# Two value-projection chunks side by side at the opening of a float32 decoder trunk, and layer 0's bias bands and residual on the weights' DMA queue

## The chip, the core and the metric

The kernel runs on one core of one Trainium2 chip. The metric is the device time of one execution in microseconds, as the median of three runs. The engines are called as the profile calls them: PE (TensorE; PEld is its weight load), ACT (ScalarE), DVE (VectorE), POOL (GpSimd) and SP (SyncE, which only issues DMAs here). A q behind an engine's name stands for its sequencer.

## The reference

One sequence of T = 256 tokens, width 2048, float32 throughout, two layers. Layer 0 has full causal attention (with 256 tokens its block-sparse form has one block), layer 1 has sliding-window attention (128 keys) with sinks and four shared key/value heads. Both add a T5 relative-position bias to the scores, and both are followed by a gated feed-forward network with a causal convolution of width 3. Each block is closed by a residual with a LayerNorm.

```python
for layer in range(2):
    if layer == 0:
        attn = moba_attention(h, moba_w_qkv[0], moba_w_o[0], rel_bias)     # 16 heads of 128
    else:
        k_band, v_band = shared_kv_bands(h, swa_w_kv)                      # 4 kv heads
        attn = swa_attention(h, swa_w_q[0], swa_sinks[0], swa_w_o[0], k_band, v_band, band_bias, band_mask)
    h = layer_norm(ALPHA * h + attn, ln_g[layer, 0], ln_b[layer, 0])
    ffn = conv_ffn(h, ffn_w_up[layer], ffn_conv_w[layer], ffn_conv_b[layer], ffn_w_down[layer])
    h = layer_norm(ALPHA * h + ffn, ln_g[layer, 1], ln_b[layer, 1])
```

The few words on the change say "layer 1's value projection" and count layers from 1; in the code it is `l == 0`, and this text says layer 0.

## The kernel before, in words

All weights lie in one DRAM tensor `wst`, cut into "halves" of 128 partitions x 1024 float32 (512 KB), in the order in which PE uses them. `load_weights` (L98) issues the next half on SP's queue into one of four `raw` buffers. A half then is split: ACT copies it to `wh` in the rounded type float32r (L128), DVE subtracts to get the low part `wl` (L157). `wh` and `wl` have four buffers each. Matmuls then add high times high, high times low and low times high, which keeps float32's accuracy. `split_upto` (L159) does the splits up to a given half, and at the end of each one issues the next raw load, which has to wait until the split has freed its buffer. `pieces` (L95) says whether a half is loaded and split whole or in two pieces of 512 columns: before, only half 0 is in pieces.

The order of work is written out by hand. `take` (L203) hands out the next half: it first runs the splits up to three halves ahead, then the jobs on an agenda (`at(n, f, ...)` puts a job n halves ahead). `step` (L197) counts one half on, and runs jobs that PE itself has (`pe_at`). So each engine's queue holds its instructions in this order and runs them in order; DMAs of SP stand in SP's order, DMAs of POOL in POOL's.

Two ways of multiplying are used. A feature unit (`ws_unit`, L293) has weights as the stationary operand: two halves, 16 K-blocks of 128, one accumulator bank of PSUM (L300 and L303). A `Moving` chunk (L337) has weights as the moving operand: 512 output columns, 16 K-blocks of 128 x 512, i.e. eight halves, with two accumulators (one for each 128 tokens) and three matmuls for each block and token tile (L353 to L355). PSUM has four `acc` banks and four `at` banks.

Layer 0's attention (L768 to L775) goes in four groups of four heads. A group begins with `v_group` (L743), the value projection of 512 columns as one `Moving` chunk, whose accumulators are evacuated into `vt` (two buffers). Then, for each head, come two feature units (q and k) and the softmax steps, which are spread over the following halves (L695 to L701).

The opening (`load_input`, L216): the input, transposed, is loaded in blocks `xc` and split into `xT`, high and low. Blocks 0 and 1 are loaded one by one on ACT's queue beside the two pieces of half 0, the others in pairs on SP's queue between the raw loads. All four tables of the bias (`bias_table`, L264) are loaded on SP as well; at half 3 PE makes the bias rows from them (L275), and POOL writes these to `ud` in DRAM (L278). `spread_bias` (L282) copies `ud` from DRAM to DRAM, with overlapping rows, into bands of four heads of 128 x 256 (512 KB each), and `load_bias` (L287) brings a band into SBUF. Both are on POOL's queue, for layer 0 at halves 4, 12, 20 and 28, and a load waits for its spread. The residual `res` (two loads of 1 MB, L244) and the LayerNorm vectors `gb` (two of 1 MB, L421) are on POOL's queue too, behind them. A tile has to be free and its data landed before an instruction that uses it runs; the framework puts in those waits, and at most eight DMAs of SP are under way, since the ninth waits for the first's semaphore.

Of the kernel before, what the change touches and what calls it, by code (L numbers as in the profile page):

```python
# [18 lines left out]
P = 128  # L19
T = 256  # L20
D = 2048
KB = D // P
# [15 lines left out]
RAW_BUFS = 4  # L38
HALF_BUFS = 4
AHEAD = HALF_BUFS - 1  # L40
HW = 1024
# [5 lines left out]
OPENING = 4  # L47
PAIRS = 6
LEAD = (16, 0)
GROUPS = ((6, 6, 6, 6, 6, 6), (6, 4, 4, 4, 4, 4))  # L50


# [25 lines left out]
def trunk(ctx: ExitStack, tc: tile.TileContext, wst, xT_in, x_in, relb, onehot, umask, sinks, conv_in, ln_g, ln_b, out):  # L78
    nc = tc.nc
# [13 lines left out]
    reach, placed = {}, {}  # L93

    def pieces(u):  # L95
        return (slice(0, HW // 2), slice(HW // 2, HW)) if u == 0 else (slice(0, HW),)

    def load_weights(behind=None):  # L98
        u = todo["load"]
        if u < n_halves:  # L100
            raws[u] = wpool.tile([P, HW], F32, name="raw")
            for j, c in enumerate(pieces(u)):
                nc.sync.dma_start(raws[u][:, c], wst[u][:, c])
                if behind:
                    behind(j)
            todo["load"] += 1
# [52 lines left out]
    def split_upto(i, behind=None):  # L159
        while todo["low"] <= min(i, n_halves - 1):  # L160
            s = todo["low"]
            high_upto(s, behind)
            if s in quad:
                quad_low(s)
                raws.pop(s - 1)
                load_weights()
            elif len(pieces(s)) == 1:
                if s - 1 in quad:
                    q = quad[s - 1]
                    nc.scalar.activation(q.uh, q.tm[:, 512:], AF.Copy)  # L170
                low_piece(s, slice(0, HW))
                if s - 1 in quad:
                    minus(q.ul, q.tm[:, 512:], q.uh.bitcast(F32))
            placed.pop(s)
            todo["low"] += 1
            if s + 1 not in quad:
                raws.pop(s)
                load_weights()
# [4 lines left out]
    def at(n, f, *a, first=False):  # L183

        fs = before.setdefault(slot["now"] + n, [])
        fs.insert(0 if first else len(fs), (f, a))
# [29 lines left out]
    def load_input(pool, tables):  # L216
        xc = pool.tile([P, KB, T], F32, name="xc", bufs=1)

        def load_x(k, n=2):
            (nc.scalar if n == 1 else nc.sync).dma_start(xc[:, k:k + n], xT_in[:, k:k + n, :])  # L220

        def split_x(k, n=2):
            ks = slice(k, k + n)
            nc.scalar.activation(xT[:, ks, 0:T], xc[:, ks], AF.Copy)
            nc.vector.tensor_tensor(out=xT[:, ks, T:2 * T], in0=xc[:, ks], in1=xT[:, ks, 0:T].bitcast(F32),
                                    op=ALU.subtract)

        load_weights(lambda j: load_x(j, 1))
        for c in range(1, RAW_BUFS):
            load_x(2 * c)  # L230
            load_weights()
        tables()
        load_x(2 * RAW_BUFS)
        split_upto(0, lambda j: split_x(j, 1))
        for c in range(1, KB // 2):
            if c + RAW_BUFS < KB // 2:
                load_x(2 * (c + RAW_BUFS))
            if c < HALF_BUFS:
                split_x(2 * c)
                split_upto(c)  # L240
            else:
                at(c - HALF_BUFS, split_x, 2 * c)

    def load_residual():  # L244
        for t in range(2):
            nc.gpsimd.dma_start(res[:, t, :], x_in[t * P:(t + 1) * P, :])

    at(24, load_residual)

    ident = const.tile([P, P], F32, name="ident")  # L250
    make_identity(nc, ident)
# [29 lines left out]

    def spread_bias(l, h0, h1):  # L282
        a = ud[l, h0:h1, :]
        nc.gpsimd.dma_start(band[l, h0:h1], bass.AP(tensor=a.tensor, offset=a.offset + P - 1,
                                                    ap=[[UL, h1 - h0], [-1, P], [1, 2 * P]]))

    def load_bias(bias, l, h0, h1):  # L287
        nc.gpsimd.dma_start(bias[:, h0:h1, :], band[l, h0:h1].rearrange("h q j -> q h j"))

    def cols(w, j):  # L290
        return w[:, j * P:(j + 1) * P]
# [411 lines left out]
    def layer_attention(l, rest, stage, turnover):  # L703
        oT = st
        kept = []
        if l:
            norm, turned = rest
            turn, low = turned
            n0 = nexth["i"]
            c = COLS[1]  # L710
            norm(c[0])
            norm(c[1])
            split_upto(n0 + 7)
            norm(c[2])

            def early(t, i):
                if t == 0 and i == 5:
                    pts = [turn(c[j]) for j in range(2)]
                    low(c[0], pts[0])
                    norm(c[3])  # L720
                    low(c[1], pts[1])
                if t == 0 and i == 7:
                    low(c[2], turn(c[2]))
                if t == 1 and i == 1:
                    low(c[3], turn(c[3]))
                if t == 1 and i < HALF_BUFS:
                    split_upto(n0 + 8 + i)

            kept = [acc_tile(), acc_tile()]
            Moving(lambda k: xT[:, k, :], KB).chunk(kept, early=early)  # L730
        pool = stage(f"att{l}")
        bias = pool.tile([P, NH, 2 * P], F32, name="bias", bufs=1)
        if l == 0:
            load_input(pool, lambda: bias_table(pool))
        else:
            nc.vector.tensor_scalar(nsk, sk, -1.0, None, op0=ALU.mult)
        for i, h in enumerate(range(0, NH, 4)):
            n = (4 + 8 * i, 4 * i)[l]
            if l == 0:
                at(n, spread_bias, l, h, h + 4)  # L740
            at(n, load_bias, bias, l, h, h + 4)

        def v_group(accs=None):  # L743
            if not accs:
                accs = [acc_tile(), acc_tile()]
                Moving(lambda k: xT[:, k, :], KB).chunk(accs)
            vt = pool.tile([P, 2, 512], F32, name="vt", bufs=1 if l else 2)

            def evac():
                for t in range(2):  # L750
                    nc.scalar.activation(vt[:, t, :], accs[t], AF.Copy)

            at(0, evac)
            return vt

        def feat_unit(name, bufs):
            acc = acc_tile()
            ws_unit(acc)
            o = pool.tile([P, T], F32, name=name, bufs=bufs)

            def evac():
                nc.scalar.activation(o, acc[:, T:2 * T], AF.Copy)
                nc.vector.tensor_tensor(out=o, in0=acc[:, 0:T], in1=o, op=ALU.add)

            at(0, evac, first=True)
            return o

        if l == 0:  # L768
            for g in range(NH // 4):
                vt = v_group()  # L770
                for j in range(4):
                    h = 4 * g + j
                    q = feat_unit("qT", 4)
                    k = feat_unit("kT", 4)
                    attention(pool, l, h, q, vt[:, :, j * P:(j + 1) * P], k, bias, oT)  # L775
        else:
            vt = v_group(kept)
            ks = [feat_unit("kT", KVH) for _ in range(KVH)]
            for h in range(NH):
                q = feat_unit("qT", 4)  # L780
                j = h // GRP
                attention(pool, l, h, q, vt[:, :, j * P:(j + 1) * P], ks[j], bias, oT)
        return project_out(lambda k: oT[:, k, :], NH, 2 * l, turnover.homes, AF.Gelu_apprx_tanh, turnover)
# [134 lines left out]
    return b.transpose(0, 2, 1, 3).reshape(-1, P, HW)  # L918


def _paired(w):

    b = w.reshape(FT, P, NCH // 2, 2, 512).transpose(2, 0, 3, 1, 4)
    seq = np.stack([b[n, k, c] for n in range(NCH // 2) for k, c in paired_order(LEAD[n], GROUPS[n])[0]])
    return seq.reshape(-1, 2, P, 512).transpose(0, 2, 1, 3).reshape(-1, P, HW)


def _stream(w_qkv, w_o0, w_kv, w_q, w_o1, w_up, w_down):
    parts = []
    q, k, v = (w_qkv[:, i * D:(i + 1) * D] for i in range(3))  # L930
    for g in range(4):
        c = slice(512 * g, 512 * (g + 1))
        parts.append(_moving(v[:, c]))
        parts.append(np.stack([_still(q[:, c]), _still(k[:, c])], 1).reshape(-1, P, HW))

    def ffn(l):
        up = w_up[l]
        parts.append(np.stack([_still(up[:, :DFF]), _still(up[:, DFF:])], 1).reshape(-1, P, HW))
        parts.append(_paired(w_down[l]))

    parts.append(_moving(w_o0))
    ffn(0)
    parts.append(_moving(w_kv[:, 512:]))
    parts.append(_still(w_kv[:, :512]).reshape(-1, P, HW))
    parts.append(_still(w_q).reshape(-1, P, HW))
    parts.append(_moving(w_o1))
    ffn(1)
    return np.concatenate(parts, 0)
# [36 lines left out]
```

## Time and profile before

| | |
|---|---|
| median of three runs | 2074.63 us (2074.5 to 2076.37) |
| the profiled execution | 2074.71 us, its span 2072.7 us |
| busy share of the span | PE 99%, PEld 86%, DVE 76%, ACT 50%, POOL 1% |
| data moved by DMA | 405.10 MB, mean 195 GB/s |
| of it on SP's queue (q1) and POOL's (q0) | 383.67 MB and 19.33 MB |
| granted TensorE clock | 0.998 of full speed |

How to read it: all times within the profile count from the span's start. A row of the timeline has the start, the busy time, engine, line, operation, output<-inputs, and in brackets the idle time of the engine ahead of it with what ended that. A row of waits has the time in all, how often, and the longest. A matmul's busy time is longer than the distance to the next one's start, since matmuls overlap in the array, so a stall of PE is read from the starts.

### The profile page before, as it was taken

The numbers are of one execution on the slowest core, as the hardware profiler recorded it, in microseconds if no ns is written. First come the engines' busy times: TensorE is split into PE (matmuls) and PEld (weight loads), VectorE is DVE, ScalarE is ACT, GpSimd is POOL, SyncE is SP. The second block draws the span as 40 slices with busy tenths as digits, with TensorE's granted clock in tenths as the row PEclk, the third lists the DMA queues.
The fourth block names the chain that finished last, engine by engine and source line by source line (L and its number), as shares of the span: only waits on it lengthen the run. The fifth ranks groups of instructions, "written<-read, shape, count | busy, mean of one in ns | idle before, by whom it ended". The sixth has DMA issues, their size and how long they took to land.

```text
span 2072.7 us, 28857 instructions
## 1 busy us (share of the span) xinstructions
PE 2058.5 (99%) x11004; PEld 1779.1 (86%) x11004; DVE 1575.2 (76%) x2310; ACT 1031.2 (50%) x1453; POOL 23.3 (1%) x36
## 2 busy tenths in 40 slices
PE   9999999999999999999999999999999999999997
PEld 7888888988888888888888888898888888888886
DVE  5555556787877877898986676788787787788886
ACT  5444444444545555454553555445545454555452
POOL 0100000000000000000000000000000000000000
PEclk9999999999999999999999999999999999999999
DMA  8855558455555555566685545736555555566563
GB/s 282 294 190 180 166 169 274 138 186 192 190 187 191 186 192 185 188 239 202 203 260 193 176 144 169 239 114 197 190 191 184 193 187 189 188 217 214 192 215 131
DMA packets 114266, 405.10 MB, mean 195 GB/s; under 512 B 15648, under 2 KB 15968, under 8 KB 112848
## 3 DMA queue, kind: packets, MB, share of 16 engines
q1 hardware_dynamic: 106832, 383.67, 56.4%
q0 software_dynamic: 7008, 19.33, 2.6%
q8 instruction: 86, 1.41, 0.3%
q14 instruction: 52, 0.43, 0.1%
q10 hardware_dynamic: 288, 0.26, 0.0%
HBM read 401.02 MB, written 6.34 MB: 197 GB/s over the span
## 4 chain that ended last, share of the span: by engine, by line
PE 99%; DVE 0%; DMA 0%; ACT 0%; SPq 0%; issue 0%
PE acc L300 38%; PE acc L303 20%; PE acc L483 6%; PE acc L484 6%; PE acc L485 6%; PE acc L353 5%; PE acc L354 5%; PE acc L355 5%; PE acc L318 1%; PE at L483 1%; PE at L484 1%; PE at L485 1%; PE acc L330 1%; PE at L653 1%; PE at L686 1%; PE at L679 1%
## 5 line engine op out<-in xcount | busy, mean ns | idle before, releaser
L157 DVE TENSOR_TENSOR wl<-raw,wh 128x1024 fp32r<-128x1024 f32 (+1 forms) x639 | 778.4, 1221 | 402.0 <-ACT wh L128 393.4
L128 ACT ACTIVATE wh<-raw 128x1024 fp32r<-128x1024 f32 (+1 forms) x639 | 674.8, 1058 | 685.4 <-issue 249.1
L300 PE MATMUL acc<-xT,wh 128*128 128x512 f32 x3456 | 872.3, 394 | 0.0
L300 PEld LDWEIGHTS acc<-xT,wh 128*128 128x128 f32 x3456 | 623.6, 189 | 112.9
L303 PEld LDWEIGHTS acc<-xT,wl 128*128 128x128 f32 x3456 | 471.4, 190 | 33.8
L303 PE MATMUL acc<-xT,wl 128*128 128x256 f32 x3456 | 481.8, 282 | 0.0
L484 PE MATMUL acc<-wl,up 128*128 128x512 f32 x360 | 140.1, 389 | 0.0
L483 PE MATMUL acc<-wh,up 128*128 128x512 f32 x360 | 140.1, 389 | 0.0
L485 PE MATMUL acc<-wh,up 128*128 128x512 f32 x360 | 140.1, 389 | 0.0
L839 DVE SCALAR_TENSOR_TENSOR work<-work,cw 128x255 f32<-128x255 f32 x172 | 83.2, 484 | 6.1
L840 DVE SCALAR_TENSOR_TENSOR work<-work,cw 128x254 f32<-128x254 f32 x172 | 83.1, 483 | 6.1
L485 PEld LDWEIGHTS acc<-wh,up 128*128 128x128 f32 x360 | 67.6, 188 | 14.1
L483 PEld LDWEIGHTS acc<-wh,up 128*128 128x128 f32 x360 | 67.6, 188 | 14.0
L484 PEld LDWEIGHTS acc<-wl,up 128*128 128x128 f32 x360 | 67.6, 188 | 13.9
L838 DVE TENSOR_SCALAR work<-work,cw 128x256 f32<-128x256 f32 x172 | 70.9, 412 | 6.2
L837 DVE TENSOR_TENSOR work<-acc,work 128x256 f32<-128x256 f32 x172 | 71.7, 417 | 1.5 <-ACT work L836 1.5
L836 ACT ACTIVATE work<-acc 128x256 f32<-128x256 f32 x172 | 62.8, 365 | 6.5 <-PE acc L330 6.5
L353 PE MATMUL acc<-wh,xT 128*128 128x512 f32 x144 | 58.7, 407 | 0.3 <-ACT wh L128 0.3
L354 PE MATMUL acc<-wl,xT 128*128 128x512 f32 x144 | 56.7, 393 | 0.8 <-DVE wl L157 0.8
L355 PE MATMUL acc<-wh,xT 128*128 128x512 f32 x144 | 56.5, 392 | 0.0
L195 ACT ACTIVATE work<-work 128x256 f32<-128x256 f32 x86 | 36.1, 420 | 38.6 <-DVE work L840 38.5
L147 ACT ACTIVATE wh<-work 128x1024 fp32r<-128x1024 f32 x24 | 25.5, 1063 | 47.0 <-DVE work L136 47.0
(197 smaller groups left out, 2210.0 us busy)
## 6 DMA issues: line engine op xcount, KB each, us to landing
raw<-in_wst_dram SPq DMA_DIRECT2D x723, 512.0 KB, 3.4
band<-ud POOLq DMA_DIRECT2D x8, 512.0 KB, 14.6
bias<-band POOLq DMA_DIRECT2D x8, 512.0 KB, 7.3
gb<-in_ln_g_dram POOLq DMA_DIRECT2D x4, 1024.0 KB, 6.3
gb<-in_ln_b_dram POOLq DMA_DIRECT2D x4, 1024.0 KB, 8.1
res<-in_x_dram POOLq DMA_DIRECT2D x2, 1024.0 KB, 7.5
out_dram<-res SPq DMA_DIRECT2D x8, 256.0 KB, 2.5
xc<-in_xT_dram SPq DMA_DIRECT2D x7, 256.0 KB, 5.7
```

What stands on the lines that cost most here:

```text
L128: nc.scalar.activation(wh[:, c], raws[s][:, c], AF.Copy)
L157: nc.vector.tensor_tensor(out=wl[:, c], in0=raws[s][:, c], in1=wh[:, c].bitcast(F32), op=ALU.subtract)
L300: nc.tensor.matmul(acc, cols(wh, j), xT[:, k, :], start=(k == 0), stop=False)
L303: nc.tensor.matmul(o, cols(wl, j), xT[:, k, 0:T], start=False, stop=(k == KB - 1))
L353: nc.tensor.matmul(acc, sh, wh, start=(k == 0), stop=False)
L354: nc.tensor.matmul(acc, sh, wl, start=False, stop=False)
L355: nc.tensor.matmul(acc, sl, wh, start=False, stop=(k == self.nk - 1))
L483: nc.tensor.matmul(acc, a[0], wh, start=key not in begun, stop=False)
L484: nc.tensor.matmul(acc, a[0], wl, start=False, stop=False)
L485: nc.tensor.matmul(acc, a[1], wh, start=False, stop=stop)
L839: nc.vector.scalar_tensor_tensor(c[:, 1:T], h[:, 0:T - 1], w[:, 1:2], c[:, 1:T], op0=ALU.mult, op1=ALU.add)
L840: nc.vector.scalar_tensor_tensor(c[:, 2:T], h[:, 0:T - 2], w[:, 0:1], c[:, 2:T], op0=ALU.mult, op1=ALU.add)
```

## The change

Layer 0's value projections of chunks 0 and 1 (columns 0 to 1023, heads 0 to 7) are made together ahead of all heads. `TWO_ORDER` gives the order of the 32 blocks: for K-blocks 0 to 11 chunk 0 and chunk 1 in turn, so that a half of the stream holds one K-block of both; then K-blocks 12 to 15 of chunk 0 (two halves), then those of chunk 1. All four `acc` banks are held. Groups 0 and 1 then use the two results, groups 2 and 3 make their own as before. The weights' order on the host (`_stream`) follows.

The opening goes with it: halves 0, 1 and 2 are loaded and split in two pieces; x blocks 2 and 3 are loaded one by one between the raw loads, 4 to 7 in pairs ahead of the tables, and the rest as jobs at halves 1, 3, 5 and 7, with the splits of x jobs at halves 1, 3 and so on to 11.

For layer 0, `spread_bias` (now at halves 8, 22, 36 and 50) and `load_bias` (at halves 12, 26, 40 and 54) and the residual loads (at halves 44 and 48) are issued by SP, in the weights' queue. POOL keeps the writes of `ud`, the LayerNorm vectors, and layer 1's spreads and loads.

```diff
+TWO_ORDER = [(k, c) for k in range(12) for c in range(2)] + [(k, c) for c in range(2) for k in range(12, KB)]
...
     def pieces(u):
-        return (slice(0, HW // 2), slice(HW // 2, HW)) if u == 0 else (slice(0, HW),)
+        return (slice(0, HW // 2), slice(HW // 2, HW)) if u < 3 else (slice(0, HW),)
...
-        load_weights(lambda j: load_x(j, 1))
-        for c in range(1, RAW_BUFS):
-            load_x(2 * c)
+        load_weights(lambda j: load_x(j, 1, nc.scalar))
+        for u in range(1, RAW_BUFS):
             load_weights()
+            if u < 3:
+                load_x(u + 1, 1)
+        load_x(4)
+        load_x(6)
         tables()
-        load_x(2 * RAW_BUFS)
         split_upto(0, lambda j: split_x(j, 1))
-        for c in range(1, KB // 2):
-            if c + RAW_BUFS < KB // 2:
-                load_x(2 * (c + RAW_BUFS))
-            if c < HALF_BUFS:
-                split_x(2 * c)
-                split_upto(c)
-            else:
-                at(c - HALF_BUFS, split_x, 2 * c)
+        for u in range(1, 3):
+            split_upto(u)
+            split_x(u + 1, 1)
+        for k in range(4, KB, 2):
+            if k > 6:
+                at(k - 7, load_x, k)
+            at(k - 3, split_x, k)
-    def load_residual():
-        for t in range(2):
-            nc.gpsimd.dma_start(res[:, t, :], x_in[t * P:(t + 1) * P, :])
-    at(24, load_residual)
+    def load_residual(t):
+        nc.sync.dma_start(res[:, t, :], x_in[t * P:(t + 1) * P, :])
+    for t in range(2):
+        at(44 + 4 * t, load_residual, t)
...
-        nc.gpsimd.dma_start(band[l, h0:h1], bass.AP(tensor=a.tensor, offset=a.offset + P - 1,
+        (nc.gpsimd if l else nc.sync).dma_start(band[l, h0:h1], bass.AP(tensor=a.tensor, offset=a.offset + P - 1,
                                                     ap=[[UL, h1 - h0], [-1, P], [1, 2 * P]]))
...
-        nc.gpsimd.dma_start(bias[:, h0:h1, :], band[l, h0:h1].rearrange("h q j -> q h j"))
+        (nc.gpsimd if l else nc.sync).dma_start(bias[:, h0:h1, :], band[l, h0:h1].rearrange("h q j -> q h j"))
...
-            n = (4 + 8 * i, 4 * i)[l]
             if l == 0:
-                at(n, spread_bias, l, h, h + 4)
-            at(n, load_bias, bias, l, h, h + 4)
+                at(8 + 14 * i, spread_bias, l, h, h + 4)
+            at((12 + 14 * i, 4 * i)[l], load_bias, bias, l, h, h + 4)
...
+        def v_two_groups():
+            accs = [[acc_tile(), acc_tile()] for c in range(2)]
+            mv, vts = Moving(lambda k: xT[:, k, :], KB), []
+            for k, c in TWO_ORDER:
+                wh, wl = mv.block()
+                for t in range(2):
+                    mv.mm(accs[c][t], k, t, wh, wl)
+                if mv.pos % 2 == 0:
+                    step()
+                if k == KB - 1:
+                    vts.append(v_evac(accs[c]))
+            return vts
...
         if l == 0:
+            vts = v_two_groups()
             for g in range(NH // 4):
-                vt = v_group()
+                vt = vts[g] if g < 2 else v_group()
```

`v_evac` is the evacuation that stood in `v_group`. On the host, `_moving_two` puts the value weights' first 1024 columns in `TWO_ORDER`.

More of the change, by code (lines that the diff above doesn't have):

```diff
@@ L217, in load_input, with load_x @@
         xc = pool.tile([P, KB, T], F32, name="xc", bufs=1)
-        def load_x(k, n=2):
-            (nc.scalar if n == 1 else nc.sync).dma_start(xc[:, k:k + n], xT_in[:, k:k + n, :])
+        def load_x(k, n=2, queue=nc.sync):
+            queue.dma_start(xc[:, k:k + n], xT_in[:, k:k + n, :])
         def split_x(k, n=2):
@@ L746, in v_group, with v_evac @@
                 Moving(lambda k: xT[:, k, :], KB).chunk(accs)
+            return v_evac(accs)
+        def v_two_groups():
[10 more added lines that the diff above has]
+            return vts
+        def v_evac(accs):
             vt = pool.tile([P, 2, 512], F32, name="vt", bufs=1 if l else 2)
@@ L918, in _moving, with _moving_two @@
     return b.transpose(0, 2, 1, 3).reshape(-1, P, HW)
+def _moving_two(w):
+    b = w.reshape(KB, P, 2, 512)
+    return np.stack([b[k, :, c] for k, c in TWO_ORDER]).reshape(-1, 2, P, 512).transpose(0, 2, 1, 3).reshape(-1, P, HW)
 def _paired(w):
@@ L932, in _stream @@
         c = slice(512 * g, 512 * (g + 1))
-        parts.append(_moving(v[:, c]))
+        if g == 0:
+            parts.append(_moving_two(v[:, 0:1024]))
+        if g > 1:
+            parts.append(_moving(v[:, c]))
         parts.append(np.stack([_still(q[:, c]), _still(k[:, c])], 1).reshape(-1, P, HW))
```

## Prediction

> **What bounds the kernel now.** First I read the page: the span, the engines' busy time and the chain that ended last.
>
> ```profile
> span 2072.7 us, 28857 instructions
> PE 2058.5 (99%) x11004; PEld 1779.1 (86%) x11004; DVE 1575.2 (76%) x2310; ACT 1031.2 (50%) x1453; POOL 23.3 (1%) x36
> PE 99%; DVE 0%; DMA 0%; ACT 0%; SPq 0%; issue 0%
> ```
>
> TensorE (PE) is the chain from one end to the other. The change adds no matmul and removes none, so it can give back only the time in which PE stands, and that is little: the span less PE's busy time is 2072.7 - 2058.5 = 14.2 us. Next I asked who PE's matmuls waited for, over the whole span.
>
> ```profile
> PE at L254 <- POOL ident masks.py:199: 1.4, 1, 1.4
> PE acc L354 <- DVE wl L157: 0.8, 1, 0.8
> PE acc L353 <- ACT wh L128: 0.3, 1, 0.3
> ```
>
> There are three waits (columns: us in all, times, longest). The first is the identity for the warm-up transposes, which the change leaves alone. The other two lie in the first value projection. A busy bar is longer than the pace, since matmuls overlap, so I read the starts in the timeline of PE instead.
>
> ```profile
> 5.17 0.80 PE L353 MATMUL acc<-wh,xT 128*128 128x512 f32 x1
> ...
> 8.59 0.40 PE L354 MATMUL acc<-wl,xT 128*128 128x512 f32 x1
> 8.82 0.39 PE L355 MATMUL acc<-wh,xT 128*128 128x512 f32 x1
> 9.49 0.50 PE L353 MATMUL acc<-wh,xT 128*128 128x512 f32 x1 [0.28 <-ACT wh L128]
> 10.75 0.51 PE L354 MATMUL acc<-wl,xT 128*128 128x512 f32 x1 [0.76 <-DVE wl L157]
> 11.09 0.39 PE L355 MATMUL acc<-wh,xT 128*128 128x512 f32 x1
> 11.32 0.39 PE L353 MATMUL acc<-wh,xT 128*128 128x512 f32 x1
> ...
> 18.57 0.39 PE L355 MATMUL acc<-wh,xT 128*128 128x512 f32 x1
> 18.89 0.81 PE L275 MATMUL at<-oh,rb 32*16 32x384 f32 x2
> 19.64 0.50 PE L353 MATMUL acc<-wh,xT 128*128 128x512 f32 x1
> ...
> 30.65 0.61 PE L300 MATMUL acc<-xT,wh 128*128 128x512 f32 x2
> ```
>
> The pace is 0.23 us a matmul (8.59 to 8.82). A half of the stream (512 KB of weights, two blocks, 12 matmuls) therefore takes 12 x 0.227 = 2.72 us. The projection runs from 5.17 to 30.65, 25.48 us, where its 96 matmuls at pace need 21.8 and the table 0.75 (18.89 to 19.64). What is left over is 2.9 us. Of this 1.1 us lies between 5.17 and 7.43, where the first five starts are 0.4 us apart or more. At the border of the first two halves there is 9.49 - 8.82 - 0.23 = 0.44, then 10.75 - 9.49 - 0.23 = 1.03, then 11.09 - 10.75 - 0.23 = 0.11, together 1.58 us. Some 0.2 us surround the table.
>
> **The change, part by part.** *The stall at the second half.* Why was that half late? These are ScalarE's (ACT) and VectorE's (DVE) rows.
>
> ```profile
> 5.50 0.63 ACT L128 ACTIVATE wh<-raw 128x512 fp32r<-128x512 f32 x1 [0.38 <-DMA raw<-in_wst_dram]
> ...
> 7.17 0.63 ACT L224 ACTIVATE xT<-xc 128x512 fp32r<-128x512 f32 x1 [0.73 <-DMA xc<-in_xT_dram]
> 8.38 1.06 ACT L128 ACTIVATE wh<-raw 128x1024 fp32r<-128x1024 f32 x1 [0.58 <-DMA raw<-in_wst_dram]
> ...
> 14.91 1.06 ACT L128 ACTIVATE wh<-raw 128x1024 fp32r<-128x1024 f32 x1 [0.61 <-DMA raw<-in_wst_dram]
> 15.88 0.61 ACT L224 ACTIVATE xT<-xc 128x512 fp32r<-128x512 f32 x1
> 18.18 1.06 ACT L128 ACTIVATE wh<-raw 128x1024 fp32r<-128x1024 f32 x1 [1.69 <-DMA raw<-in_wst_dram]
> ```
>
> ```profile
> 6.17 0.69 DVE L157 TENSOR_TENSOR wl<-raw,wh 128x512 fp32r<-128x512 f32 x1 [0.29 <-ACT wh L128]
> ...
> 16.01 1.22 DVE L157 TENSOR_TENSOR wl<-raw,wh 128x1024 fp32r<-128x1024 f32 x1 [0.37 <-ACT wh L128]
> 17.15 0.68 DVE L225 TENSOR_TENSOR xT<-xc,xT 128x512 fp32r<-128x512 f32 x1
> ```
>
> Raw half 1 came whole at 8.38, behind 256 KB of x (7.17), and its high part took 1.06 us and its low part 1.2 more; PE wanted it at 8.82 + 0.23 = 9.05. With the change half 0 holds K-block 0 of both chunks, half 1 holds K-block 1 of both, and so on. Half 1 needs no new x, since x blocks 0 and 1 come beside half 0, and it is loaded and split in two pieces of 256 KB. Its first piece stands in the weights' queue where the 256 KB of x stood, so I let it land at 7.17: high part done at 7.17 + 0.63 = 7.80, low part done 0.67 + 0.69 us after the start of the high one (rows 5.50 and 6.17), at 8.53. Both are there before 9.05. The second piece stands where the first half of the old raw 1 stood, so it lands no later than 8.38 and is done by 8.38 + 0.67 + 0.69 = 9.74; PE wants it at 9.05 + 6 x 0.227 = 10.41. The stall goes, worth **-1.58 us**. The 1.1 us at the start stay, because the first matmuls have the same pieces and order as before, and so do the 0.2 us around the table.
>
> *What is late next.* Counting the bytes queued up to and with each raw half, the new order asks for fewer: for raw 2 it is 1920 KB against 2304 before, for raw 3 it is 2560 against 3072, for raw 4 3584 against 3840 (four raw halves, eight x blocks, then the half; the tables in both). So raw 4 lands by 14.91 at the latest. Its high part, x blocks 4 and 5, its low part and their low part then run as at 14.91, 15.88, 16.01 and 17.15 and end at 17.15 + 0.68 = 17.83. PE reaches half 4 at 9.05 + 3 x 2.72 + 0.75 (table) = 17.96, and the low part of x is read by the third matmul, at 18.4. It fits, by 0.6 us; this is the tightest place. From there each half wants 512 KB of weights and 128 KB of x per 2.72 us, 241 GB/s, and this window of the opening (columns: length, busy us of PE, PEld, DVE, ACT and POOL, clock, DMA share, GB/s) moved 322:
>
> ```profile
> 5.17:30.65 25.48, 24.44 (x101) 18.87 (x100) 19.03 (x23) 15.30 (x19) 2.23 (x3) 1.00 0.93 322
> ```
>
> *The second chunk and PSUM.* Four accumulators are held instead of two. Chunk 0's pair is evacuated two halves before the end, so the first feature units find their banks free, and chunk 1's pair has four halves (two feature units) for two copies of an accumulator on ACT, which is half idle. I cost that at nothing; without this cover it would be one copy before a feature unit, some 0.6 us (the 128x512 row at 5.50).
>
> *Bias bands, residual and LayerNorm vectors.* These rows group the issues over the whole run, and the raw tile's landings alone (min, median, max) follow.
>
> ```profile
> raw<-in_wst_dram SPq DMA_DIRECT2D x723, 512.0 KB, 3.4
> band<-ud POOLq DMA_DIRECT2D x8, 512.0 KB, 14.6
> bias<-band POOLq DMA_DIRECT2D x8, 512.0 KB, 7.3
> gb<-in_ln_g_dram POOLq DMA_DIRECT2D x4, 1024.0 KB, 6.3
> gb<-in_ln_b_dram POOLq DMA_DIRECT2D x4, 1024.0 KB, 8.1
> res<-in_x_dram POOLq DMA_DIRECT2D x2, 1024.0 KB, 7.5
> ```
>
> ```profile
> DMA to landing us min/median/max: 3.0/3.4/8.7
> ```
>
> Layer 0's four spreads, four bias loads and two residual loads leave POOL's queue for SP's, where the raw loads go. A bias load waits for its spread, issued four halves (11 us) earlier, and a spread took 14.6 us at the median: on SP the wait could be 14.6 - 11 = 3.6 us, and every later raw load stands behind it. How much lead has the stream? Raw 16 was issued at 35.11, and its half began at 54.26 in the chain of waits:
>
> ```profile
> 35.11 0.33 SPq L103 DMA_DIRECT2D raw<-in_wst_dram  x1
> ```
>
> ```profile
> 54.26 1.84 PE acc L300 x8
> ```
>
> That is 19.1 us, less 1.06 + 1.22 and a handoff for the splits, so 16.7 us for the landing. A 3.6 us wait and the slowest landing of 8.7 us make 12.3, and PE does not see it. The other spreads, bias loads and residual loads (1 MB each, 7.5 us to landing) stand four halves, 11 us, or more apart, so each finds the lead whole. What a spread costs on SP's queue no row shows: below, it is a raw load's 3.4 us for the same bytes (even a shorter SP issue can't gain, PE being behind neither); above, the longest landing among spreads and bias loads, 17.7 us.
>
> ```profile
> DMA to landing us min/median/max: 4.1/10.0/17.7
> ```
>
> I take 14.6, the median of the same transfer: no cost. On POOL's queue only the two table writes and layer 0's LayerNorm vectors (2 MB) stay ahead of layer 0's FFN, so these start right behind the tables, near 24 us instead of 94. They are beside weights that have that lead; the raw loads that shared the engines with them before are within the 8.7. Cost nothing; with no lead it would be 2 MB at the opening's 322 GB/s, 6.5 us.
>
> [...]
>
> *Sum.* -1.58 us and nothing else: the span 2072.7 becomes 2071.1. The profiled execution took 2074.71 us (2.0 around its span) and becomes 2073.1. The median of the three runs, 2074.63, is within 0.1 of it, so the forecast is **2073.1 us**.
>
> **The rivals.**
>
> *Second: the opening's stall only moves (2075.9 us).* If the tables or the waits of SP let raw 4 land as late as raw 5 did, at 18.18, the low part of x block 4 ends 17.83 + (18.18 - 14.91) = 21.1, 2.7 us after PE wants it at 18.4: 2074.71 - 1.58 + 2.7 = 2075.9 us. For it: the margin is 0.6 us, and the DMA was 93% busy. Against it: 256 KB less is queued before it.
>
> *Third: slower, spreads hold the weights back (2079.5 to 2090.7 us, I take the middle, 2085).* Let a spread hold SP's queue for 17.7 us. A raw load issued up to 2.8 us (one half) behind it, with its own 3.4, lands 17.7 + 3.4 - (2.8 to 0) = 18.3 to 21.1 us after its issue, against 16.7 allowed. That is 1.6 to 4.4 us of PE's time, four times, +6.4 to +17.6 on 2074.71 - 1.58 = 2073.1. It decides once a spread holds the raw loads by more than 16.7 - 3.4 = 13.3 us. For it: the band rows. Against it: their 14.6 us are under competition with raw loads of at most 8.7 us, that is, the raw loads were held 5 us and PE never waited.
>
> *Fourth: faster by over 0.2% (under 2070.5 us).* It needs 4.2 us, more than the 2.9 us that the whole opening has over its pace; only the 1.1 us of slow first starts and the table could add to the 1.58, to 2071.8 at best.
>
> **How the numbers follow.** Forecast 0.75 (2073.1); stall moved 0.15 (2075.9); spreads 0.07 (2085); more gain 0.03, of which 0.01 beyond the bound. A measurement of this kernel can tell about 0.2%, 4.1 us, from no change. The first two cases are within that, as is most of the fourth: faster 0.01, same 0.91, slower 0.08 (the third, and 0.01 of a larger moved stall). The range: its lower end is 2071.8, all of the opening but its pace; the upper end is 2076.7, the second case with 0.8 for the runs' own spread (2074.5 to 2076.37). It leaves out the third case.
>
> **What would show it.** Right: no wait of PE for wh or wl near 9 to 11 us, starts 0.23 us apart from 7.4 to the table; the first feature unit's L300 matmuls near 5.17 + 1.1 + 192 x 0.227 + 0.75 + 0.2 = 50.8 us; raw loads landing within 16 us of issue; SP's waits for the band of a few us without a PE wait behind them. Wrong: a PE wait at 18 us (second), or PE waiting for wh or wl within 20 us of a spread's issue, at halves 8, 22, 36 and 50 (third). The prediction fails if the span differs from 2071.1 by more than the run's own spread with no PE wait to show for it.

## The result, and the profile after

| | median, us | runs | |
|---|---|---|---|
| before | 2074.71 | 21, 2074.29 to 2076.67 | |
| changed | 2072.17 | 21, 2071.61 to 2073.44 | ratio 0.9985, 95% interval 0.9979 to 0.9992 |

The changed kernel is faster, by 2.5 us between the medians. That is less than the 0.2% that the prediction took for the finest difference a measurement can tell, but the interval of the ratio excludes no change: with 21 runs each the measurement was finer than that. The forecast was 1.6 us less, 2073.1. The direction was right and the size too small by 0.9 us.

In the profile of the changed kernel, PE's waits (us in all, times, longest) have lost both rows of the second half; a wait of 0.4 us for x at the first matmul is in their place.

```profile
PE at L256 <- POOL ident masks.py:199: 1.4, 1, 1.4
PE acc L355 <- ACT xT L225: 0.4, 1, 0.4
```

The timeline of PE shows it as starts. The stall at the 13th matmul (9.49 and 10.75 before) is gone: 8.23, 8.46, 8.69 are at pace.

```profile
5.28 0.51 PE L355 MATMUL acc<-wh,xT 128*128 128x512 f32 x1 [0.36 <-ACT xT L225]
5.71 0.50 PE L356 MATMUL acc<-wl,xT 128*128 128x512 f32 x1
6.04 0.49 PE L357 MATMUL acc<-wh,xT 128*128 128x512 f32 x1
6.37 0.40 PE L355 MATMUL acc<-wh,xT 128*128 128x512 f32 x1
6.61 0.40 PE L356 MATMUL acc<-wl,xT 128*128 128x512 f32 x1
...
8.23 0.39 PE L357 MATMUL acc<-wh,xT 128*128 128x512 f32 x1
8.46 0.39 PE L355 MATMUL acc<-wh,xT 128*128 128x512 f32 x1
8.69 0.39 PE L356 MATMUL acc<-wl,xT 128*128 128x512 f32 x1
...
11.18 0.39 PE L355 MATMUL acc<-wh,xT 128*128 128x512 f32 x1
...
17.46 0.50 PE L355 MATMUL acc<-wh,xT 128*128 128x512 f32 x1
...
2058.09 0.39 PE L357 MATMUL acc<-wh,up 128*128 128x512 f32 x1
```

Two more rows of before are wanted to compare, the start of its third half and its last matmul:

```profile
13.36 0.39 PE L353 MATMUL acc<-wh,xT 128*128 128x512 f32 x1
...
2060.50 0.39 PE L355 MATMUL acc<-wh,up 128*128 128x512 f32 x1
```

The two profiled executions (2074.71 and 2071.78 us; the change's span is 2070.0) can be set side by side by these starts.

| stretch | before, us | after, us | difference |
|---|---|---|---|
| to the first matmul of the projection | 5.17 | 5.28 | +0.11 |
| its first 24 matmuls (halves 0 and 1) | 13.36 - 5.17 = 8.19 | 11.18 - 5.28 = 5.90 | -2.29 |
| on to the end of the table | 19.64 - 13.36 = 6.28 | 17.46 - 11.18 = 6.28 | 0 |
| on to the last matmul | 2060.50 - 19.64 = 2040.86 | 2058.09 - 17.46 = 2040.63 | -0.23 |
| last matmul to the span's end | 12.2 | 11.9 | -0.3 |
| around the span | 2.0 | 1.8 | -0.2 |

The gain is in the first 24 matmuls, as forecast, but it is 2.29 us there and not 1.58. Three small differences of 0.2 to 0.3 us follow elsewhere. This pair is 2.93 us apart, a little more than the medians.

### The profile page after: what moved, and what is told of

It reads as the page before. It is cut to its first block, busy times and chain, and to the rows that moved or that the text cites. A ratio compares the mean times of both kernels' runs of the same rounds, so it can differ in the third digit from the quotient of the medians.

```text
span 2070.0 us, 28868 instructions
## 1 busy us (share of the span) xinstructions
PE 2056.8 (99%) x11004; PEld 1777.8 (86%) x11004; DVE 1575.7 (76%) x2313; ACT 1032.4 (50%) x1456; POOL 14.6 (1%) x26
## 3 DMA queue, kind: packets, MB, share of 16 engines
q8 instruction: 86, 1.41, 0.3%
## 4 chain that ended last, share of the span: by engine, by line
PE 99%; DVE 0%; DMA 0%; ACT 0%; issue 0%
PE acc L302 38%; PE acc L305 20%; PE acc L485 6%; PE acc L486 6%; PE acc L487 6%; PE acc L355 5%; PE acc L356 5%; PE acc L357 5%; PE acc L320 1%; PE at L485 1%; PE at L486 1%; PE at L487 1%; PE acc L332 1%; PE at L655 1%; PE at L688 1%; PE at L681 1%
```

## Experiments

The theory at the start (A): all of the gain is in the opening, and the first matmuls' slow starts, which I had counted as the same on both sides, are part of it. The rival (B): what goes beyond 1.58 us comes from the queues. Later ones are C (slow starts and stall simply add up, as my sum had it), D and E (on the first spread). Medians are of 11 runs where not said otherwise; the kernel before had 2074.76, 2074.64 and 2074.62 in the three sets.

| kernel | median, us | ratio to before, 95% interval |
|---|---|---|
| order_alone | 2072.57 | 0.9989 (0.9980 to 0.9998) |
| order_again (the same kernel) | 2072.39 | 0.9988 (0.9980 to 0.9997) |
| queue_alone | 2074.77 | 1.0000 (0.9991 to 1.0009) |
| pieces_alone | 2073.20 | 0.9992 (0.9983 to 1.0001) |
| no_pieces | 2072.53 | 0.9989 (0.9981 to 0.9998) |
| after_again (the changed kernel) | 2072.16 | 0.9988 (0.9979 to 0.9997) |
| before_warm6 | 2074.89 | 1.0001 (0.9992 to 1.0010) |
| after_warm6 | 2073.49 | 0.9993 (0.9985 to 1.0002) |
| band0_pool | 2071.90 | 0.9987 (0.9978 to 0.9996) |
| spread_two (10 runs) | 2078.60 | 1.0019 (1.0009 to 1.0028) |

Each interval reaches some 1.9 us to either side. Differences of 0.2 to 0.4 us between the kernels with the new order therefore rest on medians of 11 and on rows, and not on these intervals.

**Which part gains.** order_alone is the change without its queues (`load_residual` issues both loads on POOL again):

```diff
-    for t in range(2):
-        at(44 + 4 * t, load_residual, t)
+    at(24, load_residual)
...
-        (nc.gpsimd if l else nc.sync).dma_start(band[l, h0:h1], bass.AP(tensor=a.tensor, offset=a.offset + P - 1,
+        nc.gpsimd.dma_start(band[l, h0:h1], bass.AP(tensor=a.tensor, offset=a.offset + P - 1,
...
-        (nc.gpsimd if l else nc.sync).dma_start(bias[:, h0:h1, :], band[l, h0:h1].rearrange("h q j -> q h j"))
+        nc.gpsimd.dma_start(bias[:, h0:h1, :], band[l, h0:h1].rearrange("h q j -> q h j"))
...
-                at(8 + 14 * i, spread_bias, l, h, h + 4)
-            at((12 + 14 * i, 4 * i)[l], load_bias, bias, l, h, h + 4)
+                at(4 + 8 * i, spread_bias, l, h, h + 4)
+            at((4 + 8 * i, 4 * i)[l], load_bias, bias, l, h, h + 4)
```

> The changed kernel with the bias bands and the residual back on POOL's queue at the old places: the order of the opening alone. Theory A (all of the gain is in the opening: the stall of 1.58 us at the second half, and on top of it slow first matmuls, which last longer in the kernel before because its stall falls into them): 2.0 to 2.9 us under the kernel before, the same as the whole change within 0.5 us. Theory B (the part beyond 1.58 us comes from the queues: POOL's software queue no longer shares the DMA engines): 1.6 us under before, 0.9 us over the whole change.

It gained 2.2 us, nearly the whole. The reason that this expectation gives for A, that the stall falls into the slow starts and lengthens them, is not in the rows: before, the starts are at pace from 7.43, ahead of the stall. A better reason comes below. queue_alone is the kernel before with the residual and bands 1 to 3 on SP at the changed kernel's places, the first band left where it was:

```diff
-        nc.gpsimd.dma_start(band[l, h0:h1], bass.AP(tensor=a.tensor, offset=a.offset + P - 1,
+        (nc.gpsimd if l or not h0 else nc.sync).dma_start(band[l, h0:h1], bass.AP(tensor=a.tensor, offset=a.offset + P - 1,
...
+                at(8 + 14 * i if i else 4, spread_bias, l, h, h + 4)
+            at((12 + 14 * i if i else 4, 4 * i)[l], load_bias, bias, l, h, h + 4)
```

> The kernel before with bias bands 1 to 3 and the residual on SP's queue at the changed kernel's places; the first band stays on POOL, since the old order wants it before SP could bring it. Theory A: within 0.4 us of before, PE's second-half stall of 1.6 us unchanged. Theory B: 0.5 to 1.1 us under before.

It gained nothing in the median, and PE's waits at the second half are all still there:

```profile
PE acc L354 <- DVE wl L157: 0.8, 1, 0.8
PE acc L353 <- ACT wh L128: 0.4, 1, 0.4
```

So the order of the opening makes the gain, and B falls for the bulk of it. Is it the pieces or the two chunks? pieces_alone is one line in the kernel before, no_pieces the same line undone in the changed one:

```diff
-        return (slice(0, HW // 2), slice(HW // 2, HW)) if u == 0 else (slice(0, HW),)
+        return (slice(0, HW // 2), slice(HW // 2, HW)) if u < 3 else (slice(0, HW),)
```

> The kernel before with halves 1 and 2 loaded and split in two pieces, nothing else. From the rows of before: raw 1's first piece lands near 7.8 and is split by 9.1, in time; raw 3, still whole and behind its pair of x blocks, is split at 15.05 and wanted at 14.7, so a stall of 0.3 us moves to the fourth half. Theory A: 1.2 us under before, up to 2 if the slow first matmuls end earlier too. Theory B: 1.2 us. If the two chunks side by side are what matters and not the pieces: under 0.5 us.

> The changed kernel with halves 1 and 2 loaded and split whole. Raw 1 then lands near 7.14 and its low part ends 7.16 + 1.06 + 1.25 = 9.47; PE wants it at 8.69 after quick first matmuls, at 9.18 after slow ones: 0.3 to 0.8 us over the changed kernel. If the pieces were what removed the stall: 1.2 us or more over.

Pieces alone gain 1.6 us in the median (the interval just reaches no change), and the stall moves to the fourth half as expected from the rows. The second matmul of that half starts at 14.39, 0.14 us later than the pace, and the next one 0.11 later still:

```profile
14.02 0.39 PE L353 MATMUL acc<-wh,xT 128*128 128x512 f32 x1
14.39 0.50 PE L354 MATMUL acc<-wl,xT 128*128 128x512 f32 x1
14.73 0.40 PE L355 MATMUL acc<-wh,xT 128*128 128x512 f32 x1
```

Without the pieces the changed kernel loses 0.37 us of its gain, as expected, by a stall of 0.36 + 0.10 us at the low part of half 1 (9.05 where 8.69 is the pace):

```profile
8.46 0.39 PE L355 MATMUL acc<-wh,xT 128*128 128x512 f32 x1
9.05 0.50 PE L356 MATMUL acc<-wl,xT 128*128 128x512 f32 x1 [0.19 <-DVE wl L158]
9.38 0.40 PE L357 MATMUL acc<-wh,xT 128*128 128x512 f32 x1
```

Either edit removes most of the stall by itself: one half in pieces comes early enough, and so does one half that needs no x ahead of it.

**Why more than 1.58 us.** The kernel before once more, twice:

> The kernel before once more, for its first ten microseconds. Its runs so far fall in two heaps, 2074.3 to 2074.9 and 2076.2 to 2076.7. Theory A: the heaps differ in when the starts of PE's matmuls go from 0.43 to 0.23 us apart; an execution near 2076.4 has them 0.43 apart until 10 us or later, one near 2074.6 until about 7.4. If the heaps come from elsewhere (DMA, the tail), the slow starts end at 7.4 in both.

> The kernel before once more, for an execution of its upper heap (2076.2 to 2076.7; about one in five). If one is met: theory A puts the 1.7 us into the opening, before the table at 18.9. Else it shows once more the second half waiting until 10.75 whatever the first matmuls' pace.

Neither execution (2074.65 and 2074.68 us) fell into the upper heap, so no profile shows where its 1.7 us lie. The clock of the runs tells what kind of time they are. In the three sets, all 12 executions of the kernel before above 2076 us, and the one of queue_alone, have a mean granted clock of 0.997; all others of these two kernels have 0.998. So has every one of the 98 executions of the changed kernel, the order alone, pieces_alone, no_pieces, band0_pool and after_warm6, while the ten of spread_two, whose profile below has 6.7 us at a granted clock of 0.50, have 0.997 or 0.996. The upper heap thus goes with a lower clock (an estimate from the 1.7 us and that clock: 3.4 us at 0.50 would lose as much), and the 98 executions of kernels without the long stall did not show it. Of the first 21 runs of the kernel before 7 lie in it, which is why the means are 2.9 us apart and the medians 2.5. Where in the execution that time is lost, and why, the runs do not show.

But before_again answers the other question. Its first matmuls got to pace earlier than in the first profile (after the third and not the fifth), and still its second half waits until 10.78, against 10.75:

```profile
6.64 0.49 PE L355 MATMUL acc<-wh,xT 128*128 128x512 f32 x1
6.97 0.39 PE L353 MATMUL acc<-wh,xT 128*128 128x512 f32 x1
7.19 0.40 PE L354 MATMUL acc<-wl,xT 128*128 128x512 f32 x1
...
9.52 0.49 PE L353 MATMUL acc<-wh,xT 128*128 128x512 f32 x1 [0.34 <-ACT wh L128]
10.78 0.50 PE L354 MATMUL acc<-wl,xT 128*128 128x512 f32 x1 [0.77 <-DVE wl L157]
```

In the kernel before the second half starts when raw 1 is split, whatever PE did until then: slow starts and stall are not two terms, they lie under the same landing. To test it I made the slow starts longer in both kernels, `WARM = 18` to `WARM = 6`:

> The kernel before with 6 warm-up transposes in place of 18, so that PE's first matmuls are slow for longer. Theory A (before, the opening is bound by the landing of raw 1: PE waits until 10.75 for the low part of half 1 however fast its first twelve matmuls were): at most 0.7 us over before. Theory C (slow first matmuls and the stall add up, as my sum had it): 1 to 2.4 us over before.

> The changed kernel with 6 warm-up transposes in place of 18. Its data is ahead of PE from the first half on, so by theory A each slow start is paid in full: 0.9 to 2.4 us over the changed kernel, more than the same edit costs the kernel before. Theory C: the same as in the kernel before, 1 to 2.4 us in both.

The kernel before lost 0.25 us (2074.89 against 2074.64), the changed one 1.33 (2073.49 against 2072.16). The slow starts went on to 11.42 in one and to 9.5 in the other; these are the last two slow starts of before_warm6 and the first behind them:

```profile
11.00 0.63 PE L353 MATMUL acc<-wh,xT 128*128 128x512 f32 x1
11.42 0.45 PE L354 MATMUL acc<-wl,xT 128*128 128x512 f32 x1
11.71 0.39 PE L355 MATMUL acc<-wh,xT 128*128 128x512 f32 x1
```

The first matmul of its second half started at 11.00 and found its data there, so 5.7 us of matmuls 0.43 us apart in place of 0.23 had cost it some 0.7 us (11.42 against 10.75) in this execution. C asked for 1 us or more in both kernels; it falls, and A holds.

**What the queues do.** The changed kernel and the order alone, side by side on one chip:

> The changed kernel once more, beside the order alone on the same chip. Theory A (queues cost and bring nothing): within 0.2 us of the order alone. Theory B (the queues bring the last 0.4 us that the medians so far show): 0.3 to 0.5 us under the order alone.

> The order alone once more, beside the whole change. Theory A: 2.2 to 2.5 us under the kernel before and within 0.2 us of the whole change. Theory B: 0.3 to 0.5 us over the whole change.

The medians differ by 0.23 us, 2072.16 and 2072.39: between the two theories, a small gain for the queues if it is one. But the profiled execution of after_again took 2073.61 us, the longest of its eleven, and shows a loss. PE's waits have a new row, on the evacuation of chunk 0 into vt, and SP's waits one for the first band (us in all, times, longest):

```profile
PE acc L302 <- ACT vt L769: 1.0, 1, 1.0
```

```profile
SPq L290 <- DMA band<-ud: 5.0, 1, 5.0
```

The timelines of ACT, SP and PE in that execution tell how:

```profile
48.99 1.06 ACT L129 ACTIVATE wh<-raw 128x1024 fp32r<-128x1024 f32 x1 [7.89 <-DMA raw<-in_wst_dram]
...
51.20 1.07 ACT L769 ACTIVATE vt<-acc 128x512 f32<-128x512 f32 x2
```

```profile
34.22 0.75 SPq L286 DMA_DIRECT2D band<-ud  x1
37.46 2.48 SPq L104 DMA_DIRECT2D raw<-in_wst_dram  x1
```

```profile
51.83 0.73 PE L302 MATMUL acc<-xT,wh 128*128 128x512 f32 x2 [0.95 <-ACT vt L769]
```

Raw 16, issued at 37.46 as the next DMA behind the spread (34.22), was there only at 48.99, 11.5 us later. ACT stood 7.9 us for it. The copies of chunk 0 into vt stand behind the high parts of raw 16 and 17 in ACT's queue, and the first feature unit needs that bank; so PE waited, 1.1 us over its pace. In the first profile of the changed kernel the same chain ended just in time. band0_pool puts the first spread and load back on POOL (with the LayerNorm vectors behind them there), nothing else:

```diff
-        (nc.gpsimd if l else nc.sync).dma_start(band[l, h0:h1], bass.AP(tensor=a.tensor, offset=a.offset + P - 1,
+        (nc.gpsimd if l or not h0 else nc.sync).dma_start(band[l, h0:h1], bass.AP(tensor=a.tensor, offset=a.offset + P - 1,
...
-        (nc.gpsimd if l else nc.sync).dma_start(bias[:, h0:h1, :], band[l, h0:h1].rearrange("h q j -> q h j"))
+        (nc.gpsimd if l or not h0 else nc.sync).dma_start(bias[:, h0:h1, :], band[l, h0:h1].rearrange("h q j -> q h j"))
```

> The changed kernel with the first band (spread and load) back on POOL's queue and the LayerNorm vectors behind it there, bands 1 to 3 and the residual on SP's. In one execution of the changed kernel SP stood 5.0 us for the first band, ACT 7.9 us for raw 16, and PE 1.0 us for the evacuation of chunk 0 behind it. Theory D (the first spread alone costs, and costs up to 1.1 us): no wait of PE for vt, raw 16 lands within 9 us, 0.1 to 0.5 us under the changed kernel's 2072.16. Theory E (that wait is chance and not the spread's): the same median, waits for vt still seen.

2071.90 us, 0.26 under after_again, and its runs lie between 2071.67 and 2072.51 where the changed kernel's reach 2073.61. ACT's copies are early, and the identity is the only wait that the waits of PE list:

```profile
46.37 1.06 ACT L769 ACTIVATE vt<-acc 128x512 f32<-128x512 f32 x2
```

```profile
PE at L256 <- POOL ident masks.py:199: 1.4, 1, 1.4
```

The starts show one more. The third matmul of half 4, which reads the low part of x, begins 0.25 us behind the pace, since raw 4 was there only at 15.35 in this execution:

```profile
17.84 0.39 PE L356 MATMUL acc<-wl,xT 128*128 128x512 f32 x1
18.32 0.50 PE L357 MATMUL acc<-wh,xT 128*128 128x512 f32 x1
```

All this fits D and does not settle it against E. The first profile of the changed kernel had no wait for vt either, and the difference of the medians, from two sets of runs, is small. The edit also moves two things at once: with the first band, the 2 MB of LayerNorm vectors go from 22.0 to 41.5 us. The vectors are a rival for the cause. In after_again ACT stood 3.4 and 2.6 us for raw 11 and 12 while they loaded, mostly before the spread was issued, and raw 16 can be issued only when raw 12 is split. In order_alone, where the vectors load at 92.5, ACT stood for neither of the two, and raw 16 went out 3.9 us earlier than in after_again (33.56 and 37.46); in band0_pool it was 34.15.

```profile
33.56 0.33 SPq L104 DMA_DIRECT2D raw<-in_wst_dram  x1
```

Issued 3.3 to 3.9 us earlier, raw 16 would have been in time even at 11.5 us from issue to landing (an estimate from these rows). So the 1.1 us are shown at most for the spread and the vectors together, and for neither alone. The next run changes the spread alone. It is meant to make a spread hold the weights' queue for longer, by issuing each spread as two DMAs of two heads; that it would hold it for twice as long, and the kernel be slower for it, was my estimate, which no run had shown:

```diff
-                at(8 + 14 * i, spread_bias, l, h, h + 4)
+                for i2 in range(0, 4, 2):
+                    at(8 + 14 * i, spread_bias, l, h + i2, h + i2 + 2)
```

> The changed kernel with each spread issued as two DMAs of two heads: the same bytes, but the slowest dimension read is 2 and not 4. [...]

It took 2078.60 us, 6.4 over the changed kernel: the same bytes in the same places. PE waited 3.9 us at the first feature unit, behind ACT's 10.3 us for raw 16, and its next sixteen matmuls took 59.72 - 54.43 = 5.29 us where a half of a feature unit takes 2.8:

```profile
54.43 3.78 PE L302 MATMUL acc<-xT,wh 128*128 128x512 f32 x8 [3.94 <-ACT vt L770]
58.01 1.91 PE L305 MATMUL acc<-xT,wl 128*128 128x256 f32 x8
59.72 1.06 PE L302 MATMUL acc<-xT,wh 128*128 128x512 f32 x3
```

```profile
51.59 1.06 ACT L129 ACTIVATE wh<-raw 128x1024 fp32r<-128x1024 f32 x1 [10.34 <-DMA raw<-in_wst_dram]
```

These are two stretches of that kernel (columns: length, busy us of PE, PEld, DVE, ACT and POOL, granted clock, DMA share, GB/s). Behind the wait the granted clock is 0.50 for 6.7 us:

```profile
53.40:60.10 6.70, 5.67 (x17) 4.85 (x18) 4.18 (x5) 5.38 (x8) 0.00 (x0) 0.50 0.76 254
60.20:90.00 29.80, 29.80 (x174) 26.30 (x173) 17.80 (x30) 13.43 (x24) 0.00 (x0) 1.00 0.54 175
```

That is the third rival of the prediction, brought about on purpose. How a spread holds the queue is in the issue of raw 16 and in the DMA share. The issue took 2.48 us in after_again and twice that here:

```profile
39.06 5.25 SPq L104 DMA_DIRECT2D raw<-in_wst_dram  x1
```

While SP stood in it, the mean busy share of the 16 DMA engines was 0.31 and 0.14. The first row is of after_again, the second of spread_two; the share is the last column but one.

```profile
38.00:40.00 2.00, 2.00 (x10) 1.66 (x9) 2.00 (x3) 1.58 (x2) 0.00 (x0) 1.00 0.31 115
```

```profile
41.00:45.00 4.00, 4.00 (x19) 3.30 (x19) 1.46 (x2) 0.25 (x1) 0.00 (x0) 1.00 0.14 50
```

With two heads in a DMA in place of four the share is about half. That speaks against the mere count of DMAs, two in place of one, as the cause; which engines were used no view shows. From the issue of the first spread to the landing of raw 16 it was 17.9 us here, 14.8 in after_again and 11.7 in the first profile of the changed kernel, so that whole time did not double.

## Why the prediction was wrong in size

*The bound.* Right: PE was the chain, and only the opening had anything to give.

*The stall at the second half.* Right in place and cause. With slow starts as in the profile of before it was right in size too: after_again had them until 7.1, and its table ended at 17.94 us where the prediction had 17.96. So close a match is partly luck: the second half began 0.1 us earlier than in the sum, and the table took 0.1 us more.

```profile
5.23 0.79 PE L355 MATMUL acc<-wh,xT 128*128 128x512 f32 x1
...
6.68 0.60 PE L355 MATMUL acc<-wh,xT 128*128 128x512 f32 x1
7.11 0.41 PE L356 MATMUL acc<-wl,xT 128*128 128x512 f32 x1
...
17.94 0.50 PE L355 MATMUL acc<-wh,xT 128*128 128x512 f32 x1
```

*The step that failed* is "The 1.1 us at the start stay, because the first matmuls have the same pieces and order as before". The instructions are the same, but their slow starts are not a constant: in the profiles of the changed kernel and of order_alone they cost 0.4 us (5.28 to 6.37 is 1.09, three matmuls at pace are 0.68), in after_again 1.0 (5.23 to 7.11 is 1.88, four at pace are 0.91). What differs is the clock. The traces' record of full clock begins 7.35 us into the span in the profile of before and 7.11 in after_again, where the matmuls are 0.43 us apart until then. In the first profile of the changed kernel it begins at 4.22, ahead of the first matmul, and there the same 18 warm-up transposes took 3.56 us where they took 4.10 in the other two:

```profile
1.36 3.56 PE L256 MATMUL at<-ident 128*128 128x128 f32 x18 [1.36 <-POOL ident masks.py:199]
```

The 0.4 us that are left there are waits for half 0's own operands: the second and third matmul (5.71, 6.04) start right behind DVE's low parts of the weights (4.96 + 0.69 = 5.65) and of x (5.57 + 0.42 = 5.99). Before, slow starts cost nothing up to that landing, since PE then stood for raw 1 in any case (before_again, before_warm6). With the stall gone each execution pays what it meets and keeps what it is spared. So the mis-sized term is the lateness of the second half. The sum gave it 1.58 us; the first 24 matmuls of the profiled pair gained 2.29, of which 1.58 is the bare stall and 0.7 the quicker starts. These 0.7 us belong to this pair of executions. How the 1.0 us that the gain of the medians has over the bare stall divides between the starts, the queues and the rest is not shown.

*What is late next.* Right: there is no wait at half 4 in the two profiles of the changed kernel, and the second rival did not come about. The place was as tight as the prediction said: in band0_pool's profile raw 4 came 0.4 us after the latest time of the sum (15.35 for 14.91), and PE stood there.

*The queues at no cost* was wrong in one place and too pessimistic in another. Wrong: I gave raw 16 a lead of 16.7 us, read off the kernel before, and forgot that the evacuation of chunk 0 waits behind it on ACT. In the changed kernel the lead is shorter. In its first profile raw 16's half begins 50.23 - 37.23 = 13.0 us after the issue and not 19.1, since the half comes 4 us earlier and the issue 2 us later. That leaves 10.6 us by the same sum:

```profile
37.23 1.41 SPq L104 DMA_DIRECT2D raw<-in_wst_dram  x1
```

```profile
50.23 1.98 PE L302 MATMUL acc<-xT,wh 128*128 128x512 f32 x8
```

The LayerNorm vectors, put at nothing as well, may have their part in the late issue (above). The copies behind raw 16 are the tighter date still. I had costed that evacuation in a paragraph of its own, where "the first feature units find their banks free". What is queued behind a waiting instruction has an earlier date than the instruction's own: in after_again raw 16's high part was ready at 50.05, before PE at its pace would have wanted it (51.83 - 1.1 = 50.7), but the copy of chunk 0 began only at 51.20. The third rival's mechanism was there, at one spread out of four and at a sixth of its price or less (1.1 us of 6.4 to 17.6). Too pessimistic: the kernels with bands 1 to 3 on SP show 1.8 us around the span, those with POOL's old queue 2.0 to 2.1 (2071.78 - 2070.0, 2073.61 - 2071.8, 2074.56 - 2072.8, 2072.30 - 2070.5 against 2074.71 - 2072.7, 2074.65 - 2072.6, 2072.21 - 2070.1, 2072.14 - 2070.0). Where that 0.25 us comes from the runs do not show. Nor do they show why the changed kernel's end after the last matmul is 0.2 to 0.3 us shorter (11.9 and 12.0 us in its two profiles, 12.2 before); queue_alone's was 0.4 longer in its profile (12.6 us).

*The chances.* I took 0.2% for what can be told and put 0.91 on no change within it. A gain of 0.12 to 0.15% was told by 21 runs. The sum itself, -1.58 us or 0.08%, said faster, and the chances should have been set by how finely the two medians can be told apart.

## What to carry to other kernels

Where an engine waits for data, the slow work ahead of the wait is free; take the wait away and that work sets the time (the longer slow starts cost 0.25 us before the change, where they just outlasted the wait, and 1.33 after it), so count what the removal is worth from when the engine could have been ready, not from the idle time in the row. When a transfer joins the queue that feeds everything, price it by how long it holds that queue (here the issue of the raw load behind it took up to 2.48 us in place of 0.33), and give each late arrival the deadline of the most urgent thing queued behind whoever waits for it, here a copy that freed a PSUM bank. And an opening bound by first landings can be mended in several ways that do not add up: two pieces in place of one whole half gave 1.6 us, two chunks side by side without the pieces 2.1 (queues included), and all of it 2.5.

## What the hardware showed that I had not expected

The first matmuls got to pace at different times in two executions of the same code. The traces' record of full clock begins at 7.35 and 6.83 us in two profiles of before, and at 4.22 and 7.11 in two of the changed kernel. (The clock column of a stretch before that reads 1.00, since the record has nothing there; the distance of the starts, 0.43 us and then 0.23, shows the change.) What sets that time the runs do not show.

Behind a single wait of 3.9 us near the first feature unit the granted clock was 0.50 in spread_two, for 6.7 us: 5.29 - 2.8 = 2.5 us on top of the wait in the first sixteen matmuls. One profile shows this.

The issue of the raw load behind the first spread on SP was longer too: 1.41 us in the first profile of the changed kernel, 2.48 in after_again and 5.25 in spread_two (rows above), where the median of the raw loads' issues is 0.33. Behind the other three spreads of that first profile it took 0.53, 0.34 and 0.40.
